# Block combinations of the down weights formed during the output projection, and the down stage's products and residual reordered

## The chip, the cores and the metric

The kernel runs on one core of a Trainium2 chip. The metric is the device time of one execution in microseconds (us), lower is better. The core has a matrix engine (TensorE: PE for its matmuls, PEld for the weight loads that overlap them), three elementwise engines (VectorE: DVE; ScalarE: ACT; GpSimd: POOL) and SyncE (SP), whose queue issues nearly all DMAs here. Each engine works through its own instructions in order; an instruction that waits holds up those behind it. That is true of SP's queue too.

## The reference, cut to what matters

One decoder layer over 1024 tokens of width 1024: sparse attention, then a gated ConvFFN, each with adaLN modulation (shift, scale, gate computed from a conditioning vector) and a residual, and a last RMSNorm.

```python
mod = cond @ ada_w[i] + ada_b[i]
sh_m, sc_m, gt_m, sh_f, sc_f, gt_f = jnp.split(mod[:, None, :], 6, axis=-1)
h = rmsnorm(x, g_mix[i]) * (1 + sc_m) + sh_m
y = dsa_mixer(h, ...)                      # attention; its last step is o @ w_o
x = x + gt_m * y
h = rmsnorm(x, g_ffn[i]) * (1 + sc_f) + sh_f
x = x + gt_f * conv_ffn(h, ...)            # (gelu(conv(u)) * v) @ w_out, D_FF = 2816
...
return rmsnorm(x, g_final)
```

The change is about `gt_f`, the gate of the FFN, and `w_out` (in the kernel `f_w_out`, 2816 x 1024), the FFN's down weights.

## The kernel before

Matmuls are made in float32 precision from three passes: each operand is split into a high part (a cast on ACT) and a low part (a subtraction on DVE or POOL: `split`), and `three` issues high x high, high x low, low x high. So every operand that PE reads costs an ACT and a DVE (or POOL) instruction first.

The stages in order, with their times in the profile: input projections and attention (0 to 421 us), the output projection `w0`/`w1`/`w2a`/`w2b` (421 to 521), the up products of the FFN (521 to 979), the down products (979 to 1214), and the last norm and stores of the last tiles (to 1224.7).

**Output projection.** A loop over eight token tiles r. `w0(r)` transposes the attention output into PSUM (`ot`) and splits it (`o_h` on ACT, `o_l` on DVE); `w1(r-1)` makes 48 matmuls into a PSUM tile `wo`, which DVE adds to `xr` (the residual x1); x1 is stored to DRAM (`x1d`) and normed (`xn`); `w2a`/`w2b(r-2)` transpose the normed tile (`xt`), modulate it (`hm`) and split it into operands of the up products (`diff`, `comb`). The PSUM pool has four tiles for `ot`, `wo` and `xt`, so a later `wo` takes the place of one that DVE has read.

**Up products.** For each of 22 chunks c of d_ff, seven products i = 0..6 (`product`) stand for eight block products in the manner of Strassen and Winograd: `prep_sum` forms sums of weight blocks on POOL (`ring<-fw,fw`), `prep_split` casts (ACT, `pr`) and subtracts (POOL, or DVE for one i). `after` combines the PSUM results into u and v, then convolution, GELU and gate (`conv`), and after every second chunk `a_sums` (`sa`, `sb`) forms the token-side block sums for the down products. All go to DRAM (`ga<-conv`, `ga<-sa`, `ga<-sb`) over SP's queue, on which the weight loads of the next chunk (`fw`, from `load_up`) stand too. Between these, `plan` runs nine pieces of the gate `gt_f`: eight times a 512 KB load of `ada_w` (`ada`) and a DVE multiply-add (`acc`), then two matmuls (`adar`).

**Down products.** Seven products again, in the order `D_ORDER`, each over eleven pairs of chunks in six groups d (five of two pairs, one of one pair) and four token tiles o: 132 matmuls a product, 924 in all. For each (i, d), n in `dseq`: `d_load` loads the token side (`da`, from `ga`) and the weight side from `f_w_out` (`db`, `tb`, `dc`); `d_sum` forms the block combination of the weights on POOL, in float32, 128 x 1024 at a time; `d_split` casts and subtracts into `ringa`, `ringb` (four n deep; `ah`, `al`, `bh`, `bl` for the last two n); `d_mm` issues the matmuls; `evict` adds the finished PSUM tile into y. The last product (i = 2) has its weights multiplied by `gt_f` on POOL in `d_sum`, because its tiles' residual is made before it. `residual` multiplies y by `gt_f` and adds x1 (`xb`), both on POOL; `square`, `finish` norm and store. Callbacks stand in a heap by a clock of planned PE time (`at_clock`, `later`); from the middle of the attention on, a scheduler decides each engine's final order.

Of the kernel before, what the change touches and what calls it, by code (L numbers as in the profile page):

```python
# [24 lines left out]
NF = DFF // P  # L25
# [15 lines left out]
ADA_M = ((0, "gt_m", 2), (1, "sh_f", 3), (2, "sc_f", 4))  # L41
GT_F = (21, 8)
# [25 lines left out]
D_ORDER = (1, 5, 6, 4, 7, 3, 2)  # L68
D_LOAD, D_SUM, D_SPLIT = 16.0, 11.0, 7.0
# [3 lines left out]
def body(ctx, tc, a):  # L73
# [950 lines left out]
    for i, nm, m in ADA_M:  # L1024
        for k in range(KD):
            at(int(ADA0 + ADA_STEP * (KD * i + k)), lambda m=m, k=k: ada_piece(m, k))
        done = ada_row if m == 2 else ada_cols
        at(int(ADA0 + ADA_STEP * KD * (i + 1)) + ADA_DONE[i],
           lambda m=m, nm=nm, done=done: ada.__setitem__(nm, done(ada[m], m, nm)))
# [215 lines left out]

    clock, events, serial = [0.0], [], [0]
# [97 lines left out]
    def gt_f_piece(k):  # L1344
        if k < KD:
            ada_piece(5, k)
        else:
            ada["gt_f"] = ada_row(ada[5], 5, "gt_f", [bank("adar") for _ in range(2)])

# [5 lines left out]
    for k in range(KD + 1):  # L1355
        plan.append((GT_F[0] + GT_F[1] * k, NF, gt_f_piece, (k,)))
# [22 lines left out]
    b_of = {1: (0, 0), 5: (0, 1), 6: (1, 1), 4: (1, 0), 7: (1, 1), 3: (1, 1), 2: (1, 0)}  # L1379
    tb, raw_a, raw_b, raw_c, ops, rings = {}, {}, {}, {}, {}, []  # L1380
# [63 lines left out]
    def evict(i, o, ps):  # L1444

        if i == 1:
            yt[o] = slot([P, D], F, f"y{o}")
            act.copy(yt[o][:, lo_t], ps)
        elif i == 5:
            act.copy(yt[o][:, hi_t], ps)  # L1450
        elif i == 6:
# [39 lines left out]
    def finish(t, parts):  # L1491
        if len(parts) == 1 and t >= 4:
            square(t, parts[0], 0)
        ss, rs = sst[t]
        if t >= 4:
# [5 lines left out]
        for cs in parts:  # L1501
            if len(parts) > 1:
                (dve if cs.start else pool).tensor_tensor(y[:, cs], y[:, cs], gfin[:, cs], op=OP.mult)
        for cs in parts:
            if len(parts) == 1:
                dve.scalar_tensor_tensor(y, y, rs[:, 1:2], gfin, op0=OP.mult, op1=OP.mult)
            elif cs.start:
                act.activation(y[:, cs], y[:, cs], AF.Copy, scale=rs[:, 1:2])
            else:
                dve.tensor_scalar(y[:, cs], y[:, cs], rs[:, 1:2], None, op0=OP.mult)  # L1510
            (nc.scalar if len(parts) > 1 and cs.start else nc.sync).dma_start(a["out"][t * P:(t + 1) * P, cs], y[:, cs])
# [12 lines left out]
    for n in range(len(dseq)):  # L1524
        at_clock(start[n] - D_LOAD, lambda n=n: d_load(n))
        at_clock(start[n] - D_SUM, lambda n=n: d_sum(n))
        at_clock(start[n] - D_SPLIT, lambda n=n: d_split(n))
    for k, i in enumerate(D_ORDER):
        if i == 7:
            for t in range(4):  # L1530
                at_clock(start[k * ND + 2] + 4.0 * t, lambda t=t: load_x1(4 + t))
        if i == 3:
            for t in range(4):
                at_clock(start[k * ND] + 4.0 * t, lambda t=t: load_x1(t))
                at_clock(start[k * ND] + 4.0 * t + 4, lambda t=t: residual(t, lo_t))
# [100 lines left out]
```

## Time and profile before

| | |
|---|---|
| time, median of 3 runs | 1223.57 us (1223.25 to 1226.93) |
| time of the profiled execution | 1226.55 us |
| its span from first to last instruction | 1224.7 us |
| PE busy | 1118.0 us, 91% |
| DVE, ACT, POOL busy | 74%, 44%, 60% |
| DMA | 153.09 MB, 125 GB/s mean |

The profiled execution is one run with its own time; its span is 1.85 us shorter than that. A matmul of 128 x 128 by 512 columns shows as 0.39 us, but they overlap, and at full clock one starts every 0.23 us. In the views below an instruction's idle time and the instruction that ended it stand in square brackets, and in the windows the granted clock is 1.00 at 2.4 GHz.

### The profile page before, as it was taken

How to read it: one execution, taken by the hardware profiler on the slowest of the kernel's cores; microseconds unless marked ns; L12 is line 12 of the kernel's file. 1: busy time of each engine (PE TensorE's matmuls, PEld its weight loads, DVE VectorE, ACT ScalarE, POOL GpSimd, SP SyncE). 2: the span in 40 equal slices, each digit the busy share in tenths (PEclk: the TensorE clock that was granted, in tenths of full speed). 3: DMA queues.
4: the chain of work that ended last, by engine and by line, in shares of the span. 5: the costliest groups of instructions: out<-in, count | busy, mean ns of one | idle time of the engine just before them, and what ended most of it. 6: DMA issues, size and time to landing. Idle time of an engine off the chain costs nothing. (4 is left out here: it accounts for less than half of the span.)

```text
span 1224.7 us, 15120 instructions
## 1 busy us (share of the span) xinstructions
PE 1118.0 (91%) x5419; PEld 914.7 (75%) x5419; DVE 902.2 (74%) x1291; ACT 541.2 (44%) x909; POOL 733.8 (60%) x422
## 2 busy tenths in 40 slices
PE   7798699878999999969999989999999999999956
PEld 6787487756877888857778768787888887878845
DVE  6776589688983235487888687868777879768885
ACT  2375676756455413254333233334333444433323
POOL 3452113042145424469989779988999719393895
PEclk8899799979999999989999999999999999999978
DMA  9634211002651223020433334243322679758312
GB/s 368 217 104 57 47 35 35 1 1 70 222 184 59 86 69 121 35 86 27 132 118 108 117 104 139 85 128 103 112 86 87 216 253 387 250 184 307 103 69 86
DMA packets 61429, 153.09 MB, mean 125 GB/s; under 512 B 5512, under 2 KB 7976, under 8 KB 61352
## 3 DMA queue, kind: packets, MB, share of 16 engines
q1 hardware_dynamic: 61208, 151.85, 37.1%
q8 instruction: 42, 0.69, 0.2%
q14 instruction: 35, 0.29, 0.1%
q10 hardware_dynamic: 144, 0.26, 0.1%
HBM read 121.94 MB, written 30.15 MB: 124 GB/s over the span
## 5 line engine op out<-in xcount | busy, mean ns | idle before, releaser
L89 PE MATMUL m<-comb,pr 128*128 128x512 f32 x1056 | 258.6, 400 | 20.0 <-ACT pr L89 10.7
L89 PEld LDWEIGHTS m<-comb,pr 128*128 128x128 f32 x1056 | 200.6, 192 | 71.3 <-ACT pr L89 15.7
L89 PE MATMUL d<-ringb,ringa 128*128 128x512 f32 x888 | 207.0, 394 | 17.2 <-DVE ringb L89 9.3
L89 POOL TENSOR_TENSOR pr<-ring,pr 128x512 fp32r<-128x512 f32 x108 | 193.2, 1803 | 30.8 <-ACT pr L89 30.6
L89 PEld LDWEIGHTS d<-ringb,ringa 128*128 128x128 f32 x888 | 168.2, 190 | 55.4 <-DVE ringb L89 11.8
L89 POOL TENSOR_TENSOR ring<-fw,fw 128x512 f32<-128x512 f32 x66 | 116.8, 1782 | 1.8
L89 ACT CAST pr<-ring 128x512 fp32r<-128x512 f32 x110 | 66.5, 618 | 64.2 <-POOL ring L89 63.7
L89 DVE TENSOR_TENSOR ringa<-da,ringa 128x1024 fp32r<-128x1024 f32 (+1 forms) x40 | 71.6, 1795 | 24.9 <-ACT ringa L89 24.9
L89 DVE SCALAR_TENSOR_TENSOR conv<-u,small,conv 128x1023 f32<-128x1023 f32 (+1 forms) x44 | 68.0, 1546 | 26.2 <-ACT conv L89 25.4
L89 DVE TENSOR_TENSOR u<-m,u 128x512 f32<-128x512 f32 x66 | 45.3, 686 | 42.9 <-PE m L89 26.1
L89 ACT CAST ringa<-da 128x1024 fp32r<-128x1024 f32 (+1 forms) x40 | 39.4, 985 | 72.7 <-PE d L89 62.5
L89 PEld LDWEIGHTS o<-vv,ptb 128*128 128x128 f32 x528 | 64.6, 192 | 7.7 <-issue 5.3
L89 POOL TENSOR_TENSOR ring<-fw 128x512 f32<-128x512 f32 x44 | 59.1, 1344 | 18.3 <-DMA fw<-in_f_w_in 17.6
L89 PE MATMUL l<-kt,q 128*128 128x512 f32 (+3 forms) x160 | 67.2, 535 | 2.9 <-ACT ptb L89 1.4
L89 ACT ACTIVATE lg<-lg,mx 128x128 f32<-128x128 f32 (+6 forms) x64 | 49.5, 774 | 45.7 <-DVE mx L89 45.2
L89 PE MATMUL o<-vv,ptb 128*128 128x128 f32 x528 | 67.1, 275 | 0.0
L89 POOL TENSOR_TENSOR mn<-near,score 128x1024 f32<-128x1024 f32 x12 | 29.3, 2450 | 51.1 <-PE pt L89 16.5
L89 PE MATMUL m<-s7h,pr 128*128 128x512 f32 x176 | 58.1, 391 | 1.3 <-POOL pr L89 1.3
L89 PE MATMUL m<-s1h,pr 128*128 128x512 f32 x176 | 58.2, 392 | 1.0 <-POOL pr L89 1.0
L89 PE MATMUL m<-s6h,pr 128*128 128x512 f32 x176 | 59.0, 397 | 0.0
L89 ACT ACTIVATE conv<-u,small 128x1024 f32<-128x1024 f32 x22 | 27.4, 1245 | 69.4 <-DVE u L89 68.0
L89 DVE SCALAR_TENSOR_TENSOR acc<-ada,cond,acc 128x1024 f32<-128x1024 f32 x28 | 44.3, 1581 | 13.8 <-DMA ada<-in_ada_w 13.6
(296 smaller groups left out, 2659.4 us busy)
## 6 DMA issues: line engine op xcount, KB each, us to landing
fw<-in_f_w_in SPq DMA_DIRECT2D x44, 512.0 KB, 4.9
da<-ga SPq DMA_DIRECT2D x35, 512.0 KB, 6.9
ada<-in_ada_w SPq DMA_DIRECT2D x32, 512.0 KB, 4.4
db<-in_f_w_out SPq DMA_DIRECT2D x30, 512.0 KB, 8.4
ga<-conv SPq DMA_DIRECT2D x33, 256.0 KB, 2.1
ga<-sa SPq DMA_DIRECT2D x22, 256.0 KB, 3.9
ga<-sb SPq DMA_DIRECT2D x22, 256.0 KB, 3.9
xt<-in_xt SPq DMA_DIRECT2D x8, 512.0 KB, 6.6
```

Source lines behind the costliest of these rows:

```text
L89: r = f(*args, **kw)
```

## The change

It does four things.

1. `gt_f` is computed during the attention (fourth entry of `ADA_M`), with its eight loads and multiply-adds; the nine pieces in the up stage are gone.
2. `w_sums(q)`, called in the output projection's loop (2, 2, 2, 1, 1, 1, 1, 1 times at r = 0..7), loads two 512 KB rows of `f_w_out`, forms the four weight combinations (for products 5, 7, 6, 4) on DVE, multiplies that of product 4 by `gt_f`, and stores each, 256 KB, to DRAM (`wt`). In the down stage `d_load` reads them from there; `d_sum`, `tb` and `dc` are gone.
3. The products' order becomes 1, 2, 5, 6, 3, 7, 4, with other combinations in `evict` (more of them on DVE).
4. `residual` multiplies on POOL and adds x1 on DVE; for token tiles 4 to 7 it is done before the last product, 4, whose weights carry the gate.

```diff
-ADA_M = ((0, "gt_m", 2), (1, "sh_f", 3), (2, "sc_f", 4))
-GT_F = (21, 8)
+ADA_M = ((0, "gt_m", 2), (1, "sh_f", 3), (2, "sc_f", 4), (3, "gt_f", 5))
...
-D_ORDER = (1, 5, 6, 4, 7, 3, 2)
-D_LOAD, D_SUM, D_SPLIT = 16.0, 11.0, 7.0
+D_ORDER = (1, 2, 5, 6, 3, 7, 4)
+D_LOAD, D_SPLIT = 16.0, 7.0
+T_AT = (2, 2, 2, 1, 1, 1, 1, 1)
...
+    def w_sums(q):
+        b1, b2 = [slot([P, D], F, f"wb{c}") for c in range(2)]
+        for c, b in enumerate((b1, b2)):
+            nc.sync.dma_start(b, a["f_w_out"][(2 * q + c) * P:(2 * q + c + 1) * P])
+        for i, o, x, y, op in ((5, b1[:, lo_t], b1[:, hi_t], b1[:, lo_t], OP.subtract),
+                               (7, b1[:, hi_t], b2[:, hi_t], b1[:, hi_t], OP.subtract),
+                               (6, b2[:, hi_t], b2[:, hi_t], b1[:, lo_t], OP.subtract),
+                               (4, b2[:, lo_t], b2[:, lo_t], b2[:, hi_t], OP.subtract)):
+            dve.tensor_tensor(o, x, y, op=op)
+            if i == 4:
+                dve.tensor_tensor(o, o, ada["gt_f"][:, lo_t], op=OP.mult)
+            nc.sync.dma_start(wt[i, q // 2][q % 2], o)
...
+        for q in range(sum(T_AT[:r]), sum(T_AT[:r + 1])):
+            w_sums(q)
...
-    for k in range(KD + 1):
-        plan.append((GT_F[0] + GT_F[1] * k, NF, gt_f_piece, (k,)))
...
-    def d_sum(n):
-
-        i, d = dseq[n]
-        b = raw_b[n]
-        if i in (5, 6):
-            pool.tensor_tensor(tb[d], b, tb[d], op=OP.subtract)
-            raw_b[n] = tb[d]
-        elif i == 4:
-            pool.tensor_tensor(b, b, tb[d], op=OP.subtract)
-        elif i == 7:
-            pool.tensor_tensor(b, b, raw_c[n], op=OP.subtract)
-        elif i == 2:
-            pool.tensor_tensor(b, b, ada["gt_f"][:, None, lo_t].to_broadcast([P, pairs(d), 512]), op=OP.mult)
...
         elif i == 7:
             y = yt[4 + o]
-            dve.tensor_tensor(y[:, lo_t], ps, y[:, lo_t], op=OP.add)
-            dve.tensor_tensor(y[:, hi_t], ps, yt[o][:, hi_t], op=OP.add)
-            later(FIN_LAG[0], lambda: residual(4 + o, slice(0, D)))
-            later(FIN_LAG[0] + 5.0 * (o + 1), lambda: finish(4 + o, (slice(0, D),)))
...
+            dve.tensor_tensor(y[:, hi_t], ps, y[:, hi_t], op=OP.add)
+            dve.tensor_tensor(z_of(o), ps, z_of(o), op=OP.add)
+            later(FIN_LAG[0] + 5.0 * o, lambda: residual(4 + o, hi_t))
+            later(FIN_LAG[0] + 5.0 * o + 2, lambda: residual(4 + o, lo_t, z_of(o)))
...
-    def residual(t, cs):
+    def residual(t, cs, z=None):
         y = yt[t][:, cs]
-        pool.tensor_tensor(y, y, ada["gt_f"][:, cs], op=OP.mult)
-        pool.tensor_tensor(y, y, xb[t][:, cs], op=OP.add)
+        pool.tensor_tensor(y, y if z is None else z, ada["gt_f"][:, cs], op=OP.mult)
+        dve.tensor_tensor(y, y, xb[t][:, cs], op=OP.add)
```

How the engines' orders move is shown at three places. First DVE in the output projection, around `xr`, the addition that frees the PSUM tile of the second tile's matmuls (`wb` are the two rows that `w_sums` loads). Before:

```order
L89 TENSOR_TENSOR xr_4247<-wo,xr_4247 128x1024
L89 TENSOR_TENSOR hm_4412<-xt,a_f 128x512 x2
L89 TENSOR_SCALAR rx<-ss 128x1
L89 TENSOR_TENSOR hm_4412<-hm_4412,sh_f_3736 128x1024
L89 TENSOR_SCALAR xn<-xr_4247,rxr 128x1024
L89 TENSOR_TENSOR diff<-hm_4412 128x512
L89 TENSOR_TENSOR o_l<-ot,o_h 128x1024
L89 TENSOR_TENSOR xr_4262<-wo,xr_4262 128x1024
```

And now, from the `o_l` ahead of the same `xr`:

```order
L89 TENSOR_TENSOR o_l<-ot,o_h 128x1024
L89 TENSOR_TENSOR wb_4419<-wb_4419 128x512
L89 TENSOR_TENSOR wb_4419<-wb_4420,wb_4419 128x512
L89 TENSOR_TENSOR wb_4420<-wb_4420,wb_4419 128x512
L89 TENSOR_TENSOR wb_4432<-wb_4432 128x512
L89 TENSOR_TENSOR wb_4420<-wb_4420 128x512
L89 TENSOR_TENSOR wb_4420<-wb_4420,gt_f 128x512
L89 TENSOR_TENSOR wb_4432<-wb_4433,wb_4432 128x512
L89 TENSOR_TENSOR xr_4304<-wo,xr_4304 128x1024
L89 TENSOR_TENSOR wb_4433<-wb_4433,wb_4432 128x512
L89 TENSOR_TENSOR hm_4521<-xt,a_f 128x512 x2
```

Seven new instructions, each behind a load, stand between `o_l` and `xr`; between this `xr` and the next there are seven more, then eight, then eight, then five a tile.

Second DVE in the up stage, around the fifth piece of the gate (`acc`); the other pieces stand at other places of their chunks. Before:

```order
L89 TENSOR_TENSOR u<-m_6194,u 128x512
L89 TENSOR_TENSOR v<-m_6194,v 128x512
L89 SCALAR_TENSOR_TENSOR acc_5512<-ada_4_6191,cond,acc_5512 128x1024
L89 TENSOR_TENSOR u<-m_6213,u 128x512
L89 SCALAR_TENSOR_TENSOR conv<-u,small,conv 128x1023
```

Now the rows of a chunk read so, all through the stage, with no such row between them:

```order
L89 TENSOR_TENSOR u<-m_6238,u 128x512
L89 TENSOR_TENSOR v<-m_6238,v 128x512
L89 TENSOR_TENSOR u<-m_6257,u 128x512
L89 SCALAR_TENSOR_TENSOR conv<-u,small,conv 128x1023
```

Third POOL near the end of the down stage (`rc` are the one-column steps of the last norm). Before:

```order
L89 TENSOR_TENSOR y_9120<-y_9120,xb_9289 128x1024
L89 TENSOR_TENSOR rc<-rc,mhalf 128x1
L89 TENSOR_TENSOR y_8522<-y_8522,xb_9451 128x512
L89 TENSOR_TENSOR db<-db,gt_f 128x1024
L89 TENSOR_SCALAR rc<-ss_9479 128x1
L89 TENSOR_TENSOR rc<-rc,mhalf 128x1
L89 TENSOR_TENSOR db<-db,gt_f 128x1024
L89 TENSOR_SCALAR rc<-ss_9526 128x1
L89 TENSOR_TENSOR db<-db,gt_f 128x1024
```

Now, up to the last norm's steps:

```order
L89 TENSOR_TENSOR y_9065<-y_9065,gt_f 128x512
L89 TENSOR_TENSOR y_9065<-z_8667,gt_f 128x512
L89 TENSOR_TENSOR y_9070<-y_9070,gt_f 128x512
L89 TENSOR_TENSOR y_9070<-z_8667,gt_f 128x512
L89 TENSOR_TENSOR y_9079<-y_9079,gt_f 128x512
L89 TENSOR_TENSOR y_9079<-z_8680,gt_f 128x512
L89 TENSOR_TENSOR y_9084<-y_9084,gt_f 128x512
L89 TENSOR_TENSOR y_9084<-z_8680,gt_f 128x512
```

No weight operand stands on POOL any more; what is left there are sixteen multiplications of y or z by the gate in the whole stage (these eight are the last) and the norms' small steps.

## Rows read from the trace of the kernel before

**Rows 1.** Windows: start:end, length, busy PE, PEld, DVE, ACT, POOL; clock, DMA share, GB/s.

```profile
421.00:521.00 100.00, 99.20 (x490) 82.88 (x488) 44.51 (x51) 25.62 (x43) 36.45 (x24) 1.00 0.19 69
608.00:778.00 170.00, 161.31 (x684) 128.62 (x683) 133.03 (x120) 59.79 (x90) 145.16 (x89) 0.98 0.34 115
815.00:985.00 170.00, 168.72 (x743) 138.63 (x742) 133.55 (x128) 68.21 (x100) 147.85 (x91) 1.00 0.37 123
980.00:1150.00 170.00, 165.93 (x728) 135.97 (x727) 137.64 (x93) 69.27 (x79) 100.14 (x38) 1.00 0.75 262
1150.00:1214.00 64.00, 50.40 (x205) 39.80 (x204) 50.74 (x30) 19.30 (x32) 58.27 (x34) 0.87 0.16 59
```

**Rows 2.** POOL's groups, 979 to 1225 us: count, busy us, mean ns, idle before.

```profile
L89 POOL TENSOR_TENSOR tb<-db,tb 128x1024 f32<-128x1024 f32 x10 | 32.3, 3254 | 28.7 <-issue 28.6
...
L89 POOL TENSOR_TENSOR db<-db,gt_f 128x1024 f32<-128x1024 f32 x5 | 15.6, 3117 | 0.1
...
L89 POOL TENSOR_TENSOR y<-y,gt_f 128x512 f32<-128x512 f32 x8 | 14.3, 1797 | 0.0
```

**Rows 3.** Timeline of PE, 1150 to 1216 us, its two long waits.

```profile
1174.37 2.07 PE L89 MATMUL d<-ringb,ringa 128*128 128x512 f32 x4 [7.53 <-ACT ringb L89]
1182.08 21.92 PE L89 MATMUL d<-ringb,ringa 128*128 128x512 f32 x85 [5.64 <-DVE ringb L89]
```

**Rows 4.** Timeline of PE, 995 to 1110 us, the longest of four waits.

```profile
1019.03 11.17 PE L89 MATMUL d<-ringb,ringa 128*128 128x512 f32 x48 [1.47 <-DVE ringb L89]
```

**Rows 5.** Timeline of SP's queue: the store of every second chunk, four of eleven.

```profile
608.13 0.32 SPq L1223 DMA_DIRECT2D ga<-conv  x1
...
778.38 0.32 SPq L1223 DMA_DIRECT2D ga<-conv  x1
...
815.70 0.32 SPq L1223 DMA_DIRECT2D ga<-conv  x1
...
970.52 0.33 SPq L1223 DMA_DIRECT2D ga<-conv  x1
```

**Rows 6.** Timeline of PE in the up stage: two of its waits.

```profile
595.93 0.88 PE L89 MATMUL m<-comb,pr 128*128 128x512 f32 x2 [2.07 <-ACT pr L89]
...
729.02 3.45 PE L89 MATMUL m<-comb,pr 128*128 128x512 f32 x8 [2.31 <-ACT pr L89]
```

**Rows 7.** Timeline of DVE: the first piece of the gate, and around the sixth.

```profile
602.38 1.79 DVE L89 TENSOR_SCALAR acc<-ada,cond 128x1024 f32<-128x1024 f32 x1
...
725.30 1.28 DVE L89 SCALAR_TENSOR_TENSOR acc<-ada,cond,acc 128x1024 f32<-128x1024 f32 x1 [3.43 <-DMA ada<-in_ada_w]
726.50 0.68 DVE L89 TENSOR_TENSOR u<-m,u 128x512 f32<-128x512 f32 x1
```

**Rows 8.** Timeline of PE in the attention, 330 to 422 us: first and last of three waits.

```profile
337.65 1.56 PE L89 MATMUL l<-kt,q 128*128 128x512 f32 x4 [0.67 <-ACT ptb L89]
...
374.37 0.98 PE L89 MATMUL pt<-ident,lg 128*128 128x128 f32 x7 [1.23 <-ACT ptb L89]
```

**Rows 9.** Timeline of PE between two tiles of the output projection.

```profile
444.85 0.39 PE L89 MATMUL wo<-woh,o_l 128*128 128x512 f32 x1
...
446.74 0.48 PE L89 MATMUL wo<-woh,o_h 128*128 128x512 f32 x1
```

**Rows 10.** Timeline of DVE at the same place.

```profile
445.28 1.22 DVE L89 TENSOR_TENSOR xr<-wo,xr 128x1024 f32<-128x1024 f32 x1 [6.25 <-PE wo L89]
```

**Rows 11.** Timeline of DVE: one kind of instruction with POOL busy, and with POOL idle.

```profile
713.52 1.77 DVE L89 TENSOR_TENSOR sb<-conv 128x512 f32<-128x512 f32 x1
...
991.71 0.68 DVE L89 TENSOR_TENSOR sa<-conv 128x512 f32<-128x512 f32 x1
```

**Rows 12.** DMA issues, 421 to 521 us: count, KB each, us to landing.

```profile
xr<-in_x SPq DMA_DIRECT2D x5, 512.0 KB, 4.1
```

**Rows 13.** Timeline of PE at the end: the last matmul.

```profile
1214.38 0.39 PE L89 MATMUL d<-bh,al 128*128 128x512 f32 x1
```

**Rows 14.** Timeline of DVE at the end: the last addition out of PSUM.

```profile
1216.49 0.68 DVE L89 TENSOR_TENSOR y<-d,y 128x512 f32<-128x512 f32 x1
```

More of the change, by code (lines that the diff above doesn't have):

```diff
@@ L1026, in body @@
             at(int(ADA0 + ADA_STEP * (KD * i + k)), lambda m=m, k=k: ada_piece(m, k))
-        done = ada_row if m == 2 else ada_cols
+        done = ada_row if m in (2, 5) else ada_cols
         at(int(ADA0 + ADA_STEP * KD * (i + 1)) + ADA_DONE[i],
@@ L1244, in a_sums @@
             nc.sync.dma_start(ga[i, q // 2][q % 2], o)
+    wt = {(i, d): dram.tile([2, P, 512], F, name=f"wt{i}_{d}") for i in range(4, 8) for d in range(ND)}
+    def w_sums(q):
[10 more added lines that the diff above has]
+            nc.sync.dma_start(wt[i, q // 2][q % 2], o)
     clock, events, serial = [0.0], [], [0]
@@ L1342, in body @@
     loaded = {(0, 0), (0, 1), (1, 1)}
[L1344 to L1348, printed above, removed]
     plan = []
@@ L1446, in evict @@
         if i == 1:
[L1447 to L1451, printed above, removed]
             if o % 2 == 0:
                 z6[o // 2] = slot([P, 2, 512], F, f"z{o // 2}")
-            dve.tensor_tensor(z_of(o), ps, yt[o][:, lo_t], op=OP.add)
-            pool.tensor_tensor(yt[o][:, hi_t], yt[o][:, hi_t], z_of(o), op=OP.add)
-        elif i == 4:
-            yt[4 + o] = slot([P, D], F, f"y{4 + o}")
-            dve.tensor_tensor(yt[4 + o][:, lo_t], ps, z_of(o), op=OP.add)
+            act.copy(z_of(o), ps)
+        elif i == 2:
+            yt[o] = slot([P, D], F, f"y{o}")
+            dve.tensor_tensor(yt[o][:, lo_t], ps, z_of(o), op=OP.add)
+            later(FIN_LAG[0] + 5.0 * o, lambda: residual(o, lo_t))
+        elif i == 5:
+            yt[4 + o] = slot([P, D], F, f"y{4 + o}")
+            act.copy(yt[4 + o][:, hi_t], ps)
+        elif i == 6:
+            y = yt[4 + o][:, hi_t]
+            dve.tensor_tensor(z_of(o), ps, z_of(o), op=OP.add)
+            dve.tensor_tensor(y, y, z_of(o), op=OP.add)
+        elif i == 3:
+            dve.tensor_tensor(yt[o][:, hi_t], ps, yt[4 + o][:, hi_t], op=OP.add)
+            later(FIN_LAG[0] + 5.0 * o, lambda: residual(o, hi_t))
+            later(FIN_LAG[0] + 5.0 * o + 4, lambda: square(o, slice(0, D), 0))
+            later(FIN_LAG[0] + 5.0 * o + 7, lambda: finish(o))
@@ new lines, in evict @@
+            dve.tensor_tensor(z_of(o), ps, z_of(o), op=OP.add)
+            later(FIN_LAG[0] + 5.0 * o, lambda: residual(4 + o, hi_t))
+            later(FIN_LAG[0] + 5.0 * o + 2, lambda: residual(4 + o, lo_t, z_of(o)))
+            later(FIN_LAG[0] + 5.0 * o + 4, lambda: square(4 + o, hi_t, 1))
+            if o == 3:
+                later(FIN_LAG[0] + 5.0 * o + 5,
+                      lambda: dve.tensor_tensor(yt[7][:, hi_t], yt[7][:, hi_t], gfin[:, hi_t], op=OP.mult))
+        else:
+            y = yt[4 + o][:, lo_t]
+            dve.tensor_tensor(y, ps, y, op=OP.add)
+            square(4 + o, lo_t, 0)
+            if o == 3:
+                dve.tensor_tensor(y, y, gfin[:, lo_t], op=OP.mult)
+            finish(4 + o)
@@ L1489, in square, with finish @@
         act.activation(sq[:, cs], yt[t][:, cs], AF.Square, scale=D ** -0.5, accum_out=sst[t][0][:, j:j + 1])
-    def finish(t, parts):
-        if len(parts) == 1 and t >= 4:
-            square(t, parts[0], 0)
+    def finish(t):
         ss, rs = sst[t]
-        if t >= 4:
+        if t < 4:
             pool.tensor_scalar(rs[:, 0:1], ss[:, 0:1], EPS, None, op0=OP.add)
@@ L1500, in finish @@
         y = yt[t]
[L1501 to L1511, printed above, removed]
+        if t < NT - 1:
+            dve.scalar_tensor_tensor(y, y, rs[:, 1:2], gfin, op0=OP.mult, op1=OP.mult)
+            nc.sync.dma_start(a["out"][t * P:(t + 1) * P], y)
+            return
+        act.activation(y[:, hi_t], y[:, hi_t], AF.Copy, scale=rs[:, 1:2])
+        dve.tensor_scalar(y[:, lo_t], y[:, lo_t], rs[:, 1:2], None, op0=OP.mult)
+        nc.scalar.dma_start(a["out"][t * P:(t + 1) * P, hi_t], y[:, hi_t])
+        nc.sync.dma_start(a["out"][t * P:(t + 1) * P, lo_t], y[:, lo_t])
     def at_clock(t, f):
@@ L1525, in body @@
         at_clock(start[n] - D_LOAD, lambda n=n: d_load(n))
-        at_clock(start[n] - D_SUM, lambda n=n: d_sum(n))
         at_clock(start[n] - D_SPLIT, lambda n=n: d_split(n))
     for k, i in enumerate(D_ORDER):
-        if i == 7:
+        if i in (5, 7):
             for t in range(4):
[L1531 to L1535, printed above, removed]
+                at_clock(start[k * ND] + 4.0 * t - 10, lambda t=t, h=i == 7: load_x1(4 * h + t))
     for p, (c, i) in enumerate(seq):
```

35 lines of the change are left out of this document (10 added, 25 removed).

## The prediction

> **What bounds the kernel now.** I read the windows by stage first. PE is busy almost throughout, and its full pace is known: in the stretch from 815 us on, 743 matmuls fill 168.72 busy us, 0.227 us each, at a granted clock of 1.00 [rows 1]. So each stage is asked one thing: how many matmuls did it issue, and how long would they take at 0.227? What is missing is what a change can win there. Between 608 and 778 us PE issued 684 matmuls in the time in which it issued 743 later [rows 1]. Between 980 and 1150 us PE is idle for 4.1 of 170 us. Between 1150 and 1214 us 205 matmuls would take 46.5 us of 64: 17.5 us are lost, while POOL is busy for 58.27 of the 64 and the clock is at 0.87, that is, part of the time at the lower level of 1.2 GHz [rows 1]. The waits of PE say for whom: at the end for ringb, the split weights [rows 3], in the up stage for pr, the split weights there [rows 6].
>
> **Gate pieces out of the up stage (A).** The store of every second chunk is a milestone. Four pairs of chunks take 170.25 us from 608.13 to 778.38, with gate pieces among them, and 154.82 us from 815.70 to 970.52, without [rows 5]: 15.4 us more for the same products. The windows agree: 743 less 684 matmuls are 59, times 0.227 gives 13.4 us [rows 1]. It is not the added work, since DVE is busy for 133.03 us in the one and 133.55 in the other. It is the place in the queue: the sixth piece kept DVE idle for 3.43 us until its load had landed, ran 1.28 us, and u, which waited behind it, was late [rows 7]; ACT's convolution steps and then its cast pr came late, and PE waited 2.31 us at 729.02 [rows 6]. With the pieces gone, the chunks should run at the later pace. The pieces stand between 602 and 795 us, so 608 to 778 holds most but not all of them. I take -14, between -8 (if a part has another cause, below) and -16.
>
> **The end of the down stage (B).** POOL combines and gates the weights in float32, 3.1 to 3.3 us for each of fifteen operations, and makes eight gate multiplications of 1.8 us [rows 2]; in the last 64 us these form a queue, and PE stands twice, for 7.53 and 5.64 us, until the operands behind it are split [rows 3]. Now the weights come gated from DRAM, so those two waits, the smaller ones and the lower clock go: 17.5 us. A new queue takes a part of the place. When product 7 ends, POOL has eight gate multiplications, 8 x 1.8 = 14.4 us, and behind each of them DVE has an addition of x1; behind these stand the last splits. Until the operands of the last two groups are needed, PE has 84 matmuls of product 4 to issue, 84 x 0.227 = 19 us. DVE's own list there (eight evictions and eight additions of 0.68, four ring splits, the last splits) is between 13 us, if it never waits for POOL, and about 22, if it is paced by POOL and slowed by it. So the new wait is between 0 and some 5 us; I take 2.5. B is -15, between -17.5 and -11.
>
> **The rest of the down stage (C).** Of the 4.1 idle us between 980 and 1150 the longest wait is one of 1.47 us for a split on DVE [rows 1, 4], in a stretch where POOL runs ten operations of 3.3 us on weights [rows 2]. Those are gone; the additional evictions on DVE (four PSUM reads of 0.68, and 16 additions) are 14 us more on an engine with 32 idle us there [rows 1]. DMA's load stays nearly as it is, 0.75 (only product 7 loses a second weight block). I take -3, between -4 and 0.
>
> **The tail (D).** The last matmul ends at 1214.38 + 0.39, but the last addition out of PSUM starts only at 1216.49 [rows 13, 14], 1.7 us later, behind other work of the end; the tail afterwards has the same steps now. I take -1.5, between -1.7 and 0.
>
> **Eight gate pieces in the attention (E).** The attention runs 24 such pieces already. PE's visible waits for them and all else there are three of 0.67 to 1.23 us [rows 8]. By these, eight more cost from 0 to some 5 us (four waits of the larger size); DVE there waits for loads as it did in the up stage, but fewer products hang on it. I take +1.5.
>
> **The combinations in the output projection (F).** Eleven calls make 55 DVE operations of 128x512. Such an operation took 0.68 us with POOL idle and 1.77 with POOL busy [rows 11]: 37 to 97 us in all. DVE is busy for 44.51 of the stage's 100 us, so 55.5 are free; POOL is busy for 36.45 [rows 1], so at a third of the dear price the sum is some 57 us, just at the edge. What can be late is xr: the last matmul of one tile's wo stands at 444.85, xr runs from 445.28 to 446.50, and the next tile's first matmul, in the place so freed, is at 446.74 [rows 9, 10]. There is only some 0.3 us of slack, and now seven or eight new operations stand ahead of each of the first four xr, each behind a load that takes about 4.1 us to land [rows 12]. Before, xr itself waited 6.25 us for its matmuls [rows 10]: this is the cover, and seven operations of 0.68, 4.8 us, fit into it, at 1.77, 12.4 us, they don't. The transfers count too: 22 loads of 512 KB and 44 stores of 256 KB are some 23 MB, 230 GB/s over the stage beside the 69 of before; the down stage moved 262 GB/s with DMA busy for 0.75 [rows 1], so some 300 would be about 0.85, and more at the first tiles, which have two calls each. On SP's queue, moreover, a store waits for its DVE operation, and the next loads, the x1 stores and the first up weights stand behind it. If each of the first four tiles is late by 1.2 us, it costs 5; by 3 to 4 us, 15. I take +5, between 0 and 15.
>
> What POOL costs DVE is where the notes speak against this change. The Trainium skill ("SBUF — State Buffer", section "Who interferes with whom") says that DVE and GpSimd share a port pair as an exclusive lock, so that the second to issue waits for the first to finish. By that rule, each new operation that meets one of POOL's could wait for the whole of it; rows 11 agree in sign (1.77 against 0.68), and the fifth rival below is what it would make of the time at its worst.
>
> **Sum.** -14 - 15 - 3 - 1.5 + 1.5 + 5 = -27. The profiled execution took 1226.55 us; less 27 that is 1199.6. It is 2.98 above the median of 1223.57, so against the median I expect 1196.6, about 1197. With each term at its better end the sum is about -39 (1184), and with each at its worse end +1, which takes six independent misses. A measurement of this kernel tells about 0.3% (3.7 us) from no change.
>
> **The rivals.**
> - *The output projection costs more.* F at 12 to 25 in place of 5: the loads arrive late in DVE's queue, xr and then the next wo with them. For it: the 0.3 us of slack [rows 9, 10] and the 0.85 of DMA. Against it: 55.5 idle us on DVE. 1204 to 1217.
> - *The gain in the up stage is smaller.* The wait of 2.07 us for pr at 595.93 [rows 6] came before the first piece ran, at 602.38 [rows 7]. If the stalls belong to the first chunks and to the loads in SP's queue, A is -2 to -4: 1207 to 1209. Against it: DVE's 3.43 us behind the load [rows 7].
> - *A new wait at the end.* The gate multiplications on POOL pace DVE's additions, and the last splits stand behind them; B is -5 if the 14.4 us meet slowed splits in full: 1207.
> - *Nothing at the end was won because the clock stays low.* If the 0.87 comes from the closing steps and not from the two waits, B is only the two waits, 13.2, and 2.5 back, -10.7: 1201, inside the forecast's range.
> - *Slower.* DVE becomes the bound of the output projection: all 55 operations at 1.77 us are 97, 42 more than DVE has idle, and the stage grows by 42: the gains without F are 32, so the time is 1234. It decides against them from a growth of 32 on, which takes a mean of (55.5 + 32) / 55 = 1.6 us an operation, and POOL is busy for only 36 of the 100 us [rows 1].
>
> **How the numbers follow.** The forecast (1184 to 1204) gets 0.69; the dear output projection 0.13; the smaller gain in the up stage 0.07; the wait at the end 0.04; slower 0.04; 0.03 stay for a pile of small losses that ends within 0.3%. The rivals between 1204 and 1213 lie mostly in the range, so it reaches from 1184, the sum of the better ends, to 1213, which leaves out the dearest part of the first rival. Faster by over 0.3%: 0.91; within: 0.03; slower: 0.06, the slower rival and what I may have overlooked.
>
> **What would show it.** A: the distance of four stores of ga<-conv is about 155 us everywhere, and the windows from 608 hold about 740 matmuls in 170 us. B: the last 64 us hold some 270 matmuls less one wait for ringb or bh, and the clock is near 1.00. C: PE idle under 2 us in 170. F: the output projection takes 100 to 110 us, wb operations are between 0.7 and 1.2 us in the mean, and PE's waits for xr stay below 3 us each. E: the attention ends within 2 us of 421. It would be wrong if PE waits over 4 us before wo in each of the first four tiles, if the chunks keep a pace of 42 us a pair without the pieces, or if PE waits for more than 5 us behind product 7.

## The result and the profile after

The changed kernel takes 1187.07 us (median of 4 runs, 1185.52 to 1190.08) against 1225.21 us before (4 runs, 1223.25 to 1226.93): a ratio of 0.9695, 95% interval 0.9669 to 0.972. Measured a second time (e12, below) it was 0.9686, 0.9653 to 0.972. The forecast was 1197 us, with a range of 1184 to 1213. The profiled execution took 1190.08 us, its span is 1188.3 us, 36.4 us less than before.

The windows of the changed kernel, with the columns of [rows 1]:

```profile
421.00:521.00 100.00, 97.84 (x488) 82.11 (x487) 79.31 (x100) 26.07 (x44) 38.72 (x24) 1.00 0.78 284
521.00:600.00 79.00, 65.74 (x269) 51.97 (x267) 67.56 (x78) 34.92 (x58) 59.12 (x33) 0.91 0.25 82
608.00:778.00 170.00, 169.03 (x746) 139.27 (x744) 128.23 (x122) 64.67 (x98) 156.37 (x98) 1.00 0.31 101
...
968.00:1180.20 212.20, 212.20 (x937) 175.39 (x935) 142.29 (x144) 88.93 (x112) 44.44 (x30) 1.00 0.62 218
```

From 608 on PE now issues 746 matmuls in 170 us, where it issued 684 [rows 1]: that is the pace of the later stretch. The whole down stage, 968 to 1180.2, is one stretch without a gap: 212.20 busy of 212.20 us, 937 matmuls, 0.2265 us each, at the full 2.4 GHz. In the output projection DVE went from 44.51 to 79.31 busy us and DMA from 0.19 to 0.78, and PE lost 1.4 us of busy time.

The stores that answer to [rows 5]:

```profile
611.17 0.32 SPq L1223 DMA_DIRECT2D ga<-conv  x1
...
766.44 0.32 SPq L1223 DMA_DIRECT2D ga<-conv  x1
...
959.40 0.33 SPq L1223 DMA_DIRECT2D ga<-conv  x1
```

Four pairs of chunks now take 155.3 us (766.44 - 611.17) in place of 170.25, and all nine pairs 348.2 in place of 362.4.

POOL's groups in the down stage (968 to 1190), which answer to [rows 2]:

```profile
L89 POOL TENSOR_TENSOR y<-y,gt_f 128x512 f32<-128x512 f32 x12 | 23.6, 1985 | 156.5 <-DVE y L89 156.5
L89 POOL TENSOR_TENSOR y<-z,gt_f 128x512 f32<-128x512 f32 x4 | 8.1, 2030 | 0.0
L89 POOL TENSOR_SCALAR rc<-ss 128x1 f32<-128x1 f32 x8 | 7.6, 952 | 15.2 <-ACT sq L89 15.0
```

POOL now waits for DVE, 156.5 us in all. Whether the new queue behind product 7 costs anything is read from DVE and PE at its end. DVE:

```profile
1152.64 1.21 DVE L89 TENSOR_TENSOR ringb<-db,ringb 128x1024 fp32r<-128x1024 f32 x1
1153.77 0.67 DVE L89 TENSOR_TENSOR y<-d,y 128x512 f32<-128x512 f32 x1
...
1160.71 2.31 DVE L89 TENSOR_TENSOR ringb<-db,ringb 128x1024 fp32r<-128x1024 f32 x1
1162.94 4.18 DVE L89 TENSOR_TENSOR y<-y,xb 128x512 f32<-128x512 f32 x5
1167.05 1.21 DVE L89 TENSOR_TENSOR al<-da,ah 128x1024 fp32r<-128x1024 f32 x1
1168.18 0.68 DVE L89 TENSOR_TENSOR y<-y,xb 128x512 f32<-128x512 f32 x1
1168.79 1.21 DVE L89 TENSOR_TENSOR bl<-db,bh 128x1024 fp32r<-128x1024 f32 x1
...
1180.58 0.69 DVE L89 TENSOR_TENSOR y<-d,y 128x512 f32<-128x512 f32 x1
```

And PE:

```profile
1169.70 0.39 PE L89 MATMUL d<-bh,ah 128*128 128x512 f32 x1
1170.05 0.50 PE L89 MATMUL d<-bl,ah 128*128 128x512 f32 x1
...
1180.16 0.39 PE L89 MATMUL d<-bh,al 128*128 128x512 f32 x1
```

The split bl is finished at 1168.79 + 1.21 = 1170.00, and PE uses it from 1170.05 on, 0.35 us after the matmul ahead of it in place of 0.23. The feared wait was there, and it was 0.1 us long: the cover, 84 matmuls in the forecast and 87 as issued, is used up to its end. At the very end, the last addition starts at 1180.58, right behind the last matmul (1180.16 + 0.39); before, 1.7 us lay between them [rows 13, 14].

What the output projection pays, DVE's groups (421 to 536 us) and PE's waits (421 to 545 us: us in total, times, longest):

```profile
L89 DVE TENSOR_TENSOR wb<-wb,wb 128x512 f32<-128x512 f32 x22 | 17.1, 777 | 1.6 <-DMA wb<-in_f_w_out 1.2
L89 DVE TENSOR_TENSOR wb<-wb 128x512 f32<-128x512 f32 x22 | 16.7, 768 | 4.2 <-DMA wb<-in_f_w_out 4.0
...
L89 DVE TENSOR_TENSOR wb<-wb,gt_f 128x512 f32<-128x512 f32 x11 | 7.6, 690 | 0.3
```

```profile
PE xt L89 <- DVE xr L89: 3.0, 1, 3.0
PE wo L89 <- DVE xr L89: 2.2, 3, 1.5
```

The 55 operations took 41.4 us, 0.75 each, near the cheap end of 0.68 to 1.77 [rows 11]. DVE waited 5.2 us in all for their loads, and PE waited 5.2 us for xr, which stands behind them; 1.3 of these us were there before.

### The profile page after: what moved, and what is told of

It is laid out like the page before. It is cut to its first block, busy times and chain, and to the rows that moved or that the text cites. A ratio compares the mean times of both kernels' runs of the same rounds, so it can differ in the third digit from the quotient of the medians.

```text
span 1188.3 us, 15292 instructions
## 1 busy us (share of the span) xinstructions
PE 1108.0 (93%) x5419; PEld 914.9 (77%) x5419; DVE 897.8 (76%) x1367; ACT 540.9 (46%) x909; POOL 619.3 (52%) x379
## 4 chain that ended last, share of the span: by engine, by line
PE 52%; DVE 8%; POOL 5%; DMA 5%; issue 3%; ACT 2%; SPq 0%; POOLq 0%; DVEq 0%; ACTq 0%
PE m L89 24%; PE d L89 18%; PE o L89 3%; PE wo L89 3%; DMA fw<-in_f_w_in 3%; POOL pr L89 3%; PE l L89 2%; DVE wb L89 2%; POOL ring L89 2%; PE pt L89 1%; DMA wb<-in_f_w_out 1%; DVE conv L89 1%; DVE xr L89 1%; DVE lg L89 0%; DMA ada<-in_ada_w 0%
## 5 line engine op out<-in xcount | busy, mean ns | idle before, releaser
L89 PE MATMUL m<-comb,pr 128*128 128x512 f32 x1056 | 252.3, 395 | 12.2 <-ACT comb L89 5.3
L89 PE MATMUL d<-ringb,ringa 128*128 128x512 f32 x888 | 202.1, 389 | 0.0
L89 POOL TENSOR_TENSOR pr<-ring,pr 128x512 fp32r<-128x512 f32 x108 | 190.7, 1780 | 19.6 <-ACT pr L89 19.4
L89 POOL TENSOR_TENSOR y<-y,gt_f 128x512 f32<-128x512 f32 x12 | 23.6, 1985 | 156.5 <-DVE y L89 156.5
L89 DVE TENSOR_TENSOR ringa<-da,ringa 128x1024 fp32r<-128x1024 f32 (+1 forms) x40 | 49.0, 1225 | 51.3 <-ACT ringa L89 51.1
L89 POOL TENSOR_TENSOR ring<-fw 128x512 f32<-128x512 f32 x44 | 61.0, 1385 | 15.8 <-DMA fw<-in_f_w_in 15.6
```

The source lines that it names most:

```text
L89: r = f(*args, **kw)
```

## The experiments

All times are medians, and each run's ratio is to the kernel before on the same chip. The table cuts the span of each profile at the same five places: the first matmul of wo, the first and the eleventh of the stores of ga<-conv shown above (one for each pair of chunks), the first and the last matmul of d. All in us, each from one profile.

| | before | changed | e1 | e2 | e3 | e4 | e5 | e6 | e7 |
|---|---|---|---|---|---|---|---|---|---|
| to first wo | 421.8 | 422.6 | 422.3 | 421.2 | 424.4 | 422.2 | 424.7 | 423.5 | 424.0 |
| to first store | 150.7 | 154.9 | 150.0 | 153.0 | 150.0 | 155.2 | 154.8 | 150.1 | 150.0 |
| ten pairs of chunks | 398.1 | 381.9 | 378.1 | 393.4 | 380.7 | 380.4 | 378.4 | 377.3 | 378.9 |
| to first d | 9.0 | 9.0 | 9.0 | 10.1 | 9.0 | 9.0 | 9.0 | 9.0 | 9.0 |
| down products | 234.8 | 211.7 | 234.8 | 211.7 | 237.3 | 221.1 | 212.8 | 222.5 | 211.7 |
| to the end | 10.3 | 8.1 | 10.5 | 7.8 | 13.3 | 8.9 | 12.2 | 12.7 | 7.8 |

**e1: the gate's pieces alone moved.** The kernel before, with

```diff
-ADA_M = ((0, "gt_m", 2), (1, "sh_f", 3), (2, "sc_f", 4))
+ADA_M = ((0, "gt_m", 2), (1, "sh_f", 3), (2, "sc_f", 4), (3, "gt_f", 5))
...
-    for k in range(KD + 1):
-        plan.append((GT_F[0] + GT_F[1] * k, NF, gt_f_piece, (k,)))
```

> The kernel before with one part of the change alone: the gate's pieces in the attention instead of the up stage. My theory (the pieces held DVE's queue in the up stage until their loads landed): four pairs of chunks at about 154 us throughout, 14 to 16 us less, and 1 to 2 us more in the attention: 1209 to 1213 us. The rival (the stalls belonged to the first chunks and to SP's queue of loads): 1222 to 1227 us.

Measured: 1207.61 us, ratio 0.987 (0.9837 to 0.9904), 16 us less. The window of the chunks, and that of the down products, which stay as slow as before:

```profile
604.80:774.80 170.00, 170.00 (x751) 140.76 (x751) 129.68 (x124) 65.92 (x99) 159.03 (x100) 1.00 0.31 101
960.00:1194.00 234.00, 215.69 (x932) 175.22 (x931) 188.66 (x122) 88.50 (x111) 158.87 (x71) 0.97 0.59 207
```

**e2: the gate's pieces alone put back.** The changed kernel, with ADA_M and the plan of before, and

```diff
-                dve.tensor_tensor(o, o, ada["gt_f"][:, lo_t], op=OP.mult)
+                dve.tensor_tensor(o, o, ada["gt_m"][:, lo_t], op=OP.mult)
```

> The changed kernel with this part alone undone: the gate's nine pieces are back in the up stage, and in the combinations of product 4 the attention's gate stands in for the FFN's, so the output is another but the work is the same. My theory: 14 to 16 us come back in the up stage, 1 to 2 go in the attention: 1199 to 1203 us. The rival: 1184 to 1189 us.

Measured: 1199.53 us, ratio 0.9801 (0.9765 to 0.9836), 12.5 us more than the changed kernel. Both agree with my theory of what the pieces cost: 16 us taken out alone, 12.5 put back, nearly all of it in the ten pairs of chunks (table).

**e3: the combinations back on POOL in the down stage.** The changed kernel, with

```diff
-        for q in range(sum(T_AT[:r]), sum(T_AT[:r + 1])):
-            w_sums(q)
...
+        if i in (5, 6):
+            pool.tensor_tensor(tb[d], b, tb[d], op=OP.subtract)
+            raw_b[n] = tb[d]
+        elif i == 4:
+            pool.tensor_tensor(b, b, tb[d], op=OP.subtract)
+            pool.tensor_tensor(b, b, ada["gt_f"][:, None, lo_t].to_broadcast([P, pairs(d), 512]), op=OP.mult)
+        elif i == 7:
+            pool.tensor_tensor(b, b, raw_c[n], op=OP.subtract)
```

> The changed kernel without the combinations in the output projection: they are made in the down stage on POOL again, in float32, 128x1024 at a time; gate early, new order and new residual stay. My theory (the sums on POOL were the bound at the end): the output projection gives back 3 to 5 us, and the down stage loses 10 to 20 us at its end, where POOL has some 35 us of sums and gates of product 4 behind 14 us of residual: 1192 to 1202 us. The rival (the new order and the addition on DVE won the down stage, the place of the sums did not): 1181 to 1184 us.

Measured: 1215.08 us, ratio 0.992 (0.9894 to 0.9946), 28 us more than the changed kernel: the direction of my theory, but more than its upper end. The output projection gives back its 5 us, and the down products lose 25.6 us and the tail 5.2. PE's two longest waits there, both in the last product, 4:

```profile
1154.39 12.77 PE L89 MATMUL d<-ringb,ringa 128*128 128x512 f32 x48 [3.75 <-DVE ringb L89]
1173.47 13.61 PE L89 MATMUL d<-ringb,ringa 128*128 128x512 f32 x47 [6.31 <-DVE ringb L89]
```

And the window of the end, 133 matmuls in 51.4 us at a clock of 0.83:

```profile
1150.00:1201.40 51.40, 37.93 (x133) 29.02 (x132) 44.64 (x30) 9.71 (x14) 40.18 (x17) 0.83 0.00 0
```

**e4: the combinations formed early, order and residual as before.** The kernel before with e1's edit, with w_sums (the gate in it for product 2 instead of 4) and the changed d_load, but with its own D_ORDER, evict and residual:

```diff
+                               (4, b2[:, hi_t], b2[:, lo_t], b2[:, hi_t], OP.subtract),
+                               (2, b2[:, lo_t], b2[:, lo_t], ada["gt_f"][:, lo_t], OP.mult)):
...
-        at_clock(start[n] - D_SUM, lambda n=n: d_sum(n))
```

> The kernel before with the gate in the attention and all combinations formed in the output projection, that of product 2 with its gate too, but with the old order of the products, the old evictions and the old residual on POOL. My theory (the place of the sums and of the gate is what counts): the down stage runs nearly without gaps as in the changed kernel, 1185 to 1191 us. The rival (order and residual): a wait of 5 to 13 us stays near the end, 1192 to 1200 us.

Measured: 1197.86 us, ratio 0.979 (0.9753 to 0.9827), 10.8 us more than the changed kernel. Here the rival is right: the place of the sums alone wins 13.7 us in the down products (234.8 in e1, 221.1 here), and the other 9.4 need the new order, evictions and residual. The window of the end:

```profile
1130.00:1188.00 58.00, 49.85 (x215) 39.64 (x214) 43.58 (x32) 22.65 (x38) 44.40 (x29) 1.00 0.22 82
```

PE's waits in the down stage (us in total, times, longest):

```profile
PE d L89 <- DVE ringb L89: 4.8, 3, 1.9
PE d L89 <- DVE bl L89: 3.4, 2, 1.7
```

Two splits on DVE, with POOL busy and with POOL idle:

```profile
1127.20 3.42 DVE L89 TENSOR_TENSOR ringb<-db,ringb 128x1024 fp32r<-128x1024 f32 x1
1156.38 1.22 DVE L89 TENSOR_TENSOR ringb<-db,ringb 128x1024 fp32r<-128x1024 f32 x1
```

And what POOL did beside the first:

```profile
1126.14 3.39 POOL L89 TENSOR_TENSOR y<-y,xb 128x1024 f32<-128x1024 f32 x1
```

POOL, which still makes the residual's multiplications and additions, is busy for 44.40 of the last 58 us, and a split that meets them takes DVE up to 3.42 us instead of 1.22. PE's five waits lie in the last product, 2. Three of them end with a slow split (2.29, 2.30 and, at half the width, 1.75 us); ahead of the splits that end the other two stands a norm for which DVE had waited 1.72 and 1.04 us for POOL:

```profile
1148.29 1.28 DVE L89 SCALAR_TENSOR_TENSOR y<-y,rc,gfin 128x1024 f32<-128x1024 f32 x1 [1.72 <-POOL rc L89]
```

**e5: only the residual's addition back on POOL.** The changed kernel, with

```diff
-        dve.tensor_tensor(y, y, xb[t][:, cs], op=OP.add)
+        pool.tensor_tensor(y, y, xb[t][:, cs], op=OP.add)
```

> The changed kernel with one line undone: the residual's addition of x1 is back on POOL. Theory one (what e4 lacked is that POOL, when it is busy at the end, slows DVE's splits and has twice the work): POOL has 16 instructions of about 2 us behind product 7 in place of 8, DVE's ringb splits there take over 2 us instead of 1.22, and PE waits for them: 1191 to 1198 us. Theory two (it was the products' order and the evictions): 1185 to 1189 us.

Measured: 1193.47 us, ratio 0.9743 (0.9719 to 0.9768), 6.4 us more. The time is that of theory one, the place is not: the down products lose 1 us and the tail 4.1. POOL is still adding x1 when the first tiles of the last product are done, and their norms stand behind that on POOL:

```profile
1168.29 6.28 POOL L89 TENSOR_TENSOR y<-y,xb 128x512 f32<-128x512 f32 x5
```

DVE's first norm waits for it, and the last additions out of PSUM stand behind the norms on DVE: the last one starts 4.5 us after the last matmul has ended at 1180.11.

```profile
1175.65 1.28 DVE L89 SCALAR_TENSOR_TENSOR y<-y,rc,gfin 128x1024 f32<-128x1024 f32 x1 [8.13 <-POOL rc L89]
...
1184.58 0.68 DVE L89 TENSOR_TENSOR y<-d,y 128x512 f32<-128x512 f32 x1
```

The addition's place is worth 5 us in these two stretches, where e4 lost 10, and mostly in the tail, where e4 lost 0.8. So e4's loss is not this line alone; order, evictions and the width of the residual's steps were not taken apart.

**e6: the combinations in the down stage, but on DVE.** e3 with dve in place of pool in those five lines:

```diff
-            pool.tensor_tensor(tb[d], b, tb[d], op=OP.subtract)
+            dve.tensor_tensor(tb[d], b, tb[d], op=OP.subtract)
```

> As e3_sums_pool (no combinations in the output projection, made in the down stage, 128x1024 at a time), but on DVE instead of POOL: 24 combinations and 6 gates of about 1.22 us, 37 us more on a DVE that is busy for 142 of 212 us there. If POOL's slow float32 operations and what they cost DVE were the loss in e3: the 5 us of the output projection come back and the end of the down stage loses 2 to 8: 1183 to 1192 us, which could beat the changed kernel. If any such work near the end is the loss: 1195 us or more.

Measured: 1196.51 us, ratio 0.9786 (0.9754 to 0.9817): 18.6 us less than on POOL (e3), 9.4 more than the changed kernel, so the second theory holds: such work near the end costs time on DVE too. The output projection's 5 us come back, and 10.8 are lost in the down products, 4.6 in the tail. In the down products one wait does it, after 76 matmuls of the last product, 4; the 23 matmuls in the 8 us from there on, at a granted clock of 0.64, would take 5.2 at 0.227:

```profile
1167.10 7.47 PE L89 MATMUL d<-ringb,ringa 128*128 128x512 f32 x20 [7.94 <-DVE ringb L89]
```

```profile
1167.00:1175.00 8.00, 7.90 (x23) 6.30 (x24) 5.86 (x8) 2.71 (x5) 0.00 (x0) 0.64 0.00 0
```

This is what the new queue costs when its cover is gone: in the changed kernel bl came just in time, and here three combinations and gates of 0.68 to 2.31 us stand behind product 7 ahead of the split that PE waits for. The tail has another cause than in e5. The last matmuls of all four tiles stand behind the late splits, so the tiles end nearly together, DVE is idle until then, and the four norms follow one another behind the last matmul. In the changed kernel the four additions start at 1172.20, 1174.01, 1175.93 and 1180.58; here three of them run back to back:

```profile
1180.73 1.89 DVE L89 TENSOR_TENSOR y<-d,y 128x512 f32<-128x512 f32 x3 [7.87 <-PE d L89]
```

**e7: the output projection without the DVE operations.** The changed kernel, its combinations not formed:

```diff
-            dve.tensor_tensor(o, x, y, op=op)
-            if i == 4:
-                dve.tensor_tensor(o, o, ada["gt_f"][:, lo_t], op=OP.mult)
```

> The changed kernel without the 55 DVE operations of the combinations: the halves are stored as they were loaded, so the output is another; the 22 loads and 44 stores stay. If the cost of the output projection (5 us by the profiles of the changed kernel and of e1) is DVE's queue: 1181 to 1184 us. If it is the transfers or SP's queue: 1186 to 1188 us.

Measured: 1182.57 us, ratio 0.9654 (0.963 to 0.9678), 4.5 us less. All of the stage's price comes with DVE's operations: with 22 loads and 44 stores still there, the stretch to the first store is back at 150.0 us. Since the stores no longer wait for those operations either, this does not part what DVE's queue loses from what SP's queue loses behind it.

**e8, e10, e11: three ways to lower that price.** The changed kernel, with in turn

```diff
-T_AT = (2, 2, 2, 1, 1, 1, 1, 1)
+T_AT = (1, 1, 1, 1, 1, 2, 2, 2)
...
-T_AT = (2, 2, 2, 1, 1, 1, 1, 1)
+T_AT = (2, 2, 2, 2, 2, 1, 0, 0)
...
-                dve.tensor_tensor(o, o, ada["gt_f"][:, lo_t], op=OP.mult)
+                pool.tensor_tensor(o, o, ada["gt_f"][:, lo_t], op=OP.mult)
```

> The changed kernel with the calls of the combinations at 1, 1, 1, 1, 1, 2, 2, 2 per tile instead of 2, 2, 2, 1, 1, 1, 1, 1. If the crowd at the first tiles costs the 5 us: PE's waits for xr there go, and the time is 1183 to 1186 us, unless the last calls press on the first up products, which would give back 2 to 5: 1187 to 1191 us. If all calls cost alike: 1186 to 1188 us.

> The changed kernel with the calls of the combinations at 2, 2, 2, 2, 2, 1, 0, 0 per tile: none at the last two tiles. If the 5 us are lost at the last tiles, whose norm and transposes the first up products wait for: 1182 to 1185 us. If they are lost at each tile's xr: the four doubled tiles cost as much as is saved, 1186 to 1190 us.

> The changed kernel with the eleven gate multiplications of product 4's combinations on POOL instead of DVE, 11 of some 1.8 us. If only DVE's queue counts: 7.6 us of its work go, and 1 to 2 us of the 5 come back, 1185 to 1186 us. If POOL's operations slow DVE's in this stage as they did at the end of the down stage: no gain or a loss, 1187 to 1192 us.

Measured: 1188.01 us, ratio 0.9714 (0.9685 to 0.9743); 1189.27 us, 0.9709 (0.9673 to 0.9746); 1187.62 us, 0.9691 (0.9654 to 0.9729). None differs from the changed kernel by more than the measurement tells. Where the calls stand did not matter in these two. In e8 PE's waits for xr fall from 5.2 to 2.6 us, but a wait for another product of DVE comes among the first up products, and the first store is no earlier, 156.0 us after the first wo:

```profile
561.18 0.50 PE L89 MATMUL m<-s7l,pr 128*128 128x512 f32 x1 [2.81 <-DVE s7l L89]
```

POOL's help brings nothing that can be measured. The combinations that remain on DVE take longer, 901 ns instead of 777, which gives back 2.7 of the 7.6 us, and PE still waits 4.5 us for xr:

```profile
L89 DVE TENSOR_TENSOR wb<-wb,wb 128x512 f32<-128x512 f32 x22 | 19.8, 901 | 2.3 <-DMA wb<-in_f_w_out 1.9
...
L89 POOL TENSOR_TENSOR wb<-wb,gt_f 128x512 f32<-128x512 f32 x11 | 16.3, 1484 | 42.3 <-DVE wb L89 26.9 <-DVE rx L89 8.4 <-PE wo L89 3.0
```

**e9: the gate's loads issued a piece earlier.** The kernel before, with

```diff
+        if k < KD - 1:
+            ada_in[k + 1] = ada_load(5, k + 1)
         if k < KD:
-            ada_piece(5, k)
+            ada_step(ada[5], ada_in[k], k)
```

> The kernel before with the gate's pieces in the up stage as they were, but each 512 KB load is issued one piece (eight products, some 22 us) ahead of its multiply-add; the scheduler then places the multiply-adds at other points of their chunks. If what cost 11 to 20 us was that DVE's queue stood until a load had landed: most of it comes back without moving the pieces, 1207 to 1214 us. If it was the DVE work itself or the load's share of SP's queue: 1220 to 1226 us.

Measured: 1223.5 us, ratio 1.0001 (0.9982 to 1.0019): nothing. But it did not test what it was made for. The scheduler moved each multiply-add up right behind its load again, and DVE still waited, 10.9 us in four waits (12.3 in four before):

```profile
652.70 1.69 DVE L89 SCALAR_TENSOR_TENSOR acc<-ada,cond,acc 128x1024 f32<-128x1024 f32 x1 [3.10 <-DMA ada<-in_ada_w]
681.75 1.29 DVE L89 SCALAR_TENSOR_TENSOR acc<-ada,cond,acc 128x1024 f32<-128x1024 f32 x1 [3.65 <-DMA ada<-in_ada_w]
```

PE's waits for pr (600 to 800 us) are nearly those of before, 7.7 us in four there:

```profile
PE m L89 <- ACT pr L89: 6.9, 4, 2.8
```

Nor are all of these waits of one kind. Just ahead of the one of 1.83 us at 637.73, in the kernel before, ACT's cast pr had stood for the load of the weights that it casts, fw, not for a piece of the gate:

```profile
637.06 0.62 ACT L89 CAST pr<-fw 128x512 fp32r<-128x512 f32 x1 [4.97 <-DMA fw<-in_f_w_in]
```

**e12: the changed kernel again**, beside e9 to e11.

> The changed kernel itself, as the measure for the three beside it on the same chip: 1185 to 1190 us by all theories.

Measured: 1186.68 us, ratio 0.9686 (0.9653 to 0.972).

## Why the prediction was right, and where it was off

The forecast had the time in its range and its terms in their places; its sum, -27, was some 10 us short of the 36.4 between the profiles. The terms, in differences of the profiles (table, and its first wo for E). A term read from two profiles is rough: in the eleven profiles with the gate early the ten pairs took 377.3 to 381.9 us, in the three with the pieces 392.9 to 398.1.

- **A, -14 forecast, -16.1 measured** over the ten pairs (-14.2 over the nine of [rows 5]). Rival two is out: e1 and e2 move nothing else, and get 16 and 12.5 us. That the pieces cost this is shown; the way in which they do is only in part. The window from 608 lacks 14.7 us (170 less 684 x 0.227): 8.7 are idle, the rest is matmuls that took longer than 0.227. Two of PE's long waits for pr follow a piece that had waited for its load, the one at 729.02 [rows 6, 7] and one of 2.92 us at 684.05 behind a piece that stood 3.48 us. Each took more than itself (below). But others, as 1.83 us at 637.73, have no such piece just ahead. There the cast pr had stood 4.97 us for its own weights (e9), and a wait of that kind is left in the changed kernel, 1.79 us at 600.69, in place of the 2.07 that rival two named; on that one the rival was right. And the argument that it is not the added work fails: DVE's 133.03 and 133.55 busy us belong to 684 and 743 matmuls, so for the same products DVE has some 10 us more to do where the pieces are. Whether the pieces cost by their waits, by their work or by what both do to SP's queue, and whether early loads would do as well as the move, was not settled; e9 left the waits nearly as they were.
- **B and C, -18 forecast, -23.1 measured.** This is the term that was mis-sized, by the 2.5 us kept for the wait behind product 7, by taking 3 of the 4.1 idle us of the second window, and by the 1.5 us that neither window counts. The down stage had 234.8 us for matmuls that take 212. Rival four is out: the clock is at 1.00 to the end of the last product. The reason given was incomplete: "those two waits, the smaller ones and the lower clock go", because the weights come gated from DRAM, holds only with the new order, evictions and residual. The sums' place alone wins 13.7 us (e4 against e1); the new order, evictions and residual alone, with the sums on POOL, win nothing and lose 2.5 (e3 against e1; its last product takes two steps on POOL, a combination and the gate, where that of before takes one); both win 23.
- **The new wait, 0 to 5 us forecast, 0.1 measured.** bl came at 1170.00 for a use at 1170.05. DVE's own list took 21.6 us from 1148.36 on, near the 22 of its dear end; the 13 of its cheap end was too low, since sixteen operations of 0.68 and four splits of 1.22 are 15.8 without the last splits. Rival three was one small delay away, and e6 shows its price: a wait of 7.94 us, and the lower clock behind it.
- **D, -1.5 forecast, -2.2 measured.** The addition is on time now, which is 1.7 of it. The forecast took the steps behind it to be the same, and they are not quite: a multiplication by gfin that stood on POOL among the last norm's steps (1.26 us) is on DVE now (0.69); whether that is the other 0.5 was not tested. What e5's tail of 12.2 us waits for is POOL's leftovers; in e3 and e6 (13.3 and 12.7) it is four tiles that end together, with DVE idle for 6.76 and 7.87 us just before.
- **E, +1.5 forecast, +0.8 measured** in this profile. From profile to profile the first wo of kernels with 32 pieces lay between 422.2 and 425.6, with 24 pieces between 421.2 and 422.6; so the price is some 2 us, within what was kept for it.
- **F, +5 forecast, +4.2 measured** to the first store, 4.5 by e7. The slack of 0.3 us at xr was read rightly, and PE's waits for xr, 3.9 us more than before, are where the stage pays in the changed kernel. The transfers, which the forecast counted too, cost nothing that can be seen.
- **The slower rival** needed a mean of 1.6 us an operation; it was 0.75, so most of them ran as fast as beside an idle POOL.

The Trainium skill ("SBUF — State Buffer", section "Who interferes with whom") says that, outside DVE's 2-port modes, a DVE instruction contends with GpSimd only where it has two SBUF inputs and GpSimd's instruction reads SBUF, and that the one that issues first goes through while the other waits. The trace of the changed kernel agrees: y<-d,y, which reads PSUM and one SBUF tile, took 0.67 us at 1153.77 beside POOL's work, and ringb<-db,ringb, with two SBUF inputs, took 2.31 us at 1160.71, behind a gate multiplication that had started at 1160.19. At 1152.64 the same split took 1.21 us, and it was POOL's multiplication that took longer, 2.37 us instead of 1.30; the two starts lie 0.01 us apart, so the trace does not tell which was issued first. POOL's rows there:

```profile
1149.13 1.30 POOL L89 TENSOR_TENSOR y<-y,gt_f 128x512 f32<-128x512 f32 x1 [10.55 <-DVE y L89]
...
1152.63 2.37 POOL L89 TENSOR_TENSOR y<-y,gt_f 128x512 f32<-128x512 f32 x1
...
1160.19 1.75 POOL L89 TENSOR_TENSOR y<-y,gt_f 128x512 f32<-128x512 f32 x1
```

So here the additions out of PSUM stayed cheap on DVE beside POOL's work, and POOL's work was dear where it stood beside the splits.

## What to carry to other kernels

Elementwise work that does not depend on the stage's data belongs where the engine that makes it has idle time and little waits directly behind it: the same combinations cost some 5 us in the output projection, 15 in the down stage on DVE (e6, 10.8 and 4.6), and 31 there on POOL (e3, 25.6 and 5.2). To price a stall, multiply the matmuls of a window by their time at the full pace, and take the whole difference to the window's length, waits and clock together, over the whole stage. And look at what the helper engine still has to do when the last product begins: there, the new order, evictions and residual, with which it is finished early, were worth 9 us beside the 14 of the work removed. Which of the three does it was not taken apart.

## What the runs showed of the hardware

Some of PE's waits cost more than their length. In the kernel before, 36 matmuls followed the wait of 2.92 us in 10 us, at a granted clock of 0.83, so in part at 1.2 GHz; they take 8.2 us at 0.227. Before it, and from 694 on, the clock was 1.00:

```profile
660.00:681.00 21.00, 21.00 (x94) 17.16 (x92) 17.28 (x16) 5.44 (x9) 18.57 (x11) 1.00 0.45 150
684.00:694.00 10.00, 9.95 (x36) 7.58 (x37) 7.43 (x5) 3.43 (x6) 9.85 (x6) 0.83 0.09 31
694.00:706.00 12.00, 12.00 (x55) 9.62 (x53) 7.77 (x9) 4.81 (x8) 8.22 (x7) 1.00 0.38 129
```

The wait of 2.31 us was followed by 0.83 too, that of 1.83 us by 1.00. And in e4, five waits of 1.2 to 1.9 us, 8.2 in all, left the clock at 1.00. A length from which on this happens can't be read from these traces: in the changed kernel, a wait of 1.79 us at 600.69 was followed by 37 matmuls in 10 us at 0.83.

```profile
600.69 0.73 PE L89 MATMUL m<-comb,pr 128*128 128x512 f32 x2 [1.79 <-ACT pr L89]
```

```profile
600.70:610.70 10.00, 10.00 (x37) 8.11 (x38) 6.74 (x5) 3.90 (x5) 10.00 (x7) 0.83 0.11 42
```
